# Attention in an encoder kernel: probabilities copied by DMA and transposed in float32r

## The chip, the cores and the metric

The kernel runs on one core of a Trainium2 chip. The metric is the device time of one execution in microseconds; the median of three runs before the change is 1133.47 us (1133.27 to 1133.87). The engines are named as in the profile: PE (matmuls), PEld (PE's weight loads), DVE (vector), ACT (scalar, activations), POOL (GpSimd), SP (issues most of the DMAs).

## The reference, cut to what matters

Two layers on 512 tokens of 1024 features, all float32. Layer 0 mixes with gated linear attention, layer 1 with softmax attention, and each is followed by a gated MLP with a width-3 convolution. The change lies in the softmax attention: 8 query heads of 128 features share 2 key/value heads, and 512 tokens are swept in 128-query blocks.

```
def block(q_blk):
    s = jnp.einsum('bkgqd,bksd->bkgqs', q_blk, k).astype(jnp.float32) * scale
    p = jax.nn.softmax(s, axis=-1).astype(v.dtype)
    return jnp.einsum('bkgqs,bksd->bkgqd', p, v)

o = lax.map(block, qb)
...
return o @ w_out
```

## The kernel before

Activations stay transposed in SBUF (features on partitions, 512 tokens along the row). Nearly every matmul is made of three float32r matmuls: each operand is split into a rounded high part (an ACT copy into a float32r tile) and a low part (a DVE subtraction of the high part from the value), and high x high, high x low and low x high are accumulated (`mm3`). Weights come in 1 MB pieces from DRAM through SP's queue into `raw` and are split into `wh` and `wl` by ACT and DVE; in the attention some low parts are made by an accumulating DMA on POOL's queue instead.

In `attention` the keys, the first pair of query heads and the values are projected first. Then a loop runs over t; step t does, in this order:

- `scores` of block t, where a block is one head and 128 queries: three matmuls into a bank tagged `s` (two banks), the row maximum `mx` and its negative scaled value `nb` on DVE, and the exponential on ACT, which writes `p` (128x512 float32, tag `t`, six buffers) and its row sums;
- some steps of the projection of the next pair of query heads (`qpair`, generators placed by the tables `Q_STEPS` and `Q_READY`) and of the output projection (`out_steps`, placed by `O_STEPS`);
- `turn` of block t - LAG: four 128x128 transposes on PE from `p` into a bank tagged `pt` (two banks); the high part `pth` by ACT, the low part `ptl` by DVE;
- `shares` of block t: the reciprocal of the row sums and the scaling of `p`, both on DVE;
- `mix` of the two blocks that end at t - LAG2, when that block is the second of a pair: twelve matmuls of 256 columns into `po`, and after a whole head the split of the result into `oT`.

LAGS is (4, 6). The tile framework then schedules the recorded instructions by its own cost estimates and writes each engine's order; so what stands in the order of the loop may be moved on an engine. It also chooses buffers and adds the waits. An instruction that waits on an engine holds back those behind it on that engine's queue; a DMA issued on ACT's queue is one of these.

`pe.transpose` makes the data the stationary operand and moves an identity matrix through it.

Of the kernel before, what the change touches and what calls it, by code (L numbers as in the profile page):

```python
# [8 lines left out]
F32 = mybir.dt.float32  # L9
F32R = mybir.dt.float32r  # L10
U8 = mybir.dt.uint8
AF = mybir.ActivationFunctionType
ALU = mybir.AluOpType

P = 128
S = 512
D = 1024
KC = D // P
NT = S // P
# [9 lines left out]

GATE_STEPS, GATE_LAG = (1, 3, 5, 7, 10, 12, 15, 17), 2  # L30

LAGS = (4, 6)

Q_STEPS = {1: (0, (4,) * 4), 2: (4, (3, 3, 2, 2, 2, 2, 2)), 3: (11, (2,) * 8)}
Q_READY = {1: (4, (3, 3, 2, 1, 1, 0, 1)), 2: (11, (3, 2, 2, 1, 1, 1, 0, 1)), 3: (19, (3, 2, 2, 1, 1, 1, 0, 1))}

O_STEPS = (22, 23, 25, 27, 29, 31, 32, 33, 34, 35, 36, 37)


PC_NORM = 0  # L40
# [6 lines left out]
def hybrid_encoder_kernel(  # L47
# [20 lines left out]
    nc = tc.nc  # L68
    pe, act, dve, pool, sync = nc.tensor, nc.scalar, nc.vector, nc.gpsimd, nc.sync
    mm = pe.matmul  # L70

    cp = ctx.enter_context(tc.tile_pool(name="cp", bufs=1))
    sp = ctx.enter_context(tc.tile_pool(name="sp", bufs=1))
# [4 lines left out]
    def nm(s):  # L78
        uid[0] += 1
        return f"{s}{uid[0]}"  # L80
# [3 lines left out]
    def bank(tag, n):  # L84
        return pp.tile([P, S], F32, tag=tag, bufs=PS[tag], name=nm(n))
# [4 lines left out]
    def big(dt, n):  # L90
        return pair("g", 22, dt, n)

    def tmp(tag, n, w=S):
        return sp.tile([P, w], F32, tag=tag, bufs={"u": 4, "t": 6, "sq": 3}[tag], name=nm(n))

    def tiny(w, n, tag="tiny"):
        return sp.tile([P, 8], F32, tag=tag, bufs={"tiny": 36, "tiny2": 4}[tag], name=nm(n))[:, :w]
# [73 lines left out]
        sync.dma_start(raw[c // 4][:, r], w_vg[c // 4, :, r])  # L171
        W.raw[id(w_vg), c // 4] = raw[c // 4]

    ident = cp.tile([P, P], F32, name="ident")
    make_identity(nc, ident)

    two = tmp("u", "two")
    dve.memset(two[:, :P], 2.0 ** -5)
# [85 lines left out]
    def mm3(ps, wh, wl, mh, ml, start, stop):  # L264

        mm(ps, wh, mh, start=start, stop=False)  # L266
        mm(ps, wh, ml, start=False, stop=False)  # L267
        mm(ps, wl, mh, start=False, stop=stop)  # L268
# [367 lines left out]
    def attention(norm, nxt):  # L636
# [22 lines left out]
        def roped(i, wcol, by, keep, tag="acc"):  # L659

            pa, pb = bank(tag, "A"), bank(tag, "B")
            yield from feature_steps(*W.half(qk_order[i], 0), norm.hl, pa)
            yield from feature_steps(*W.half(qk_order[i], 1), norm.hl, pb)
            qa, qb = tmp("sq", "qa"), tmp("sq", "qb")
            act.activation(qa, pa, AF.Square)
            act.activation(qb, pb, AF.Square)
            dve.tensor_tensor(qa, qa, qb, ALU.add)
            yield
            wa, wb = prm[:, wcol : wcol + 1], prm[:, wcol + 1 : wcol + 2]
            t = [tmp("u", "rt") for _ in range(4)]  # L670
            rt = ((t[0], pa, wa, cos), (t[2], pa, wa, sin), (t[1], pb, wb, sin), (t[3], pb, wb, cos))

            def turned(n):
                dst, src, w, tab = rt[n]
                dve.scalar_tensor_tensor(dst, src, w, tab, ALU.mult, ALU.mult)

            turned(0)
            yield
            sc = scale_tok(qa, by, keep)
            yield  # L680
            turned(1)
            yield
            turned(2)
            yield
            yield
            turned(3)
            yield
            res = big(F32, "ry")
            res = [res[:, :S], res[:, S:]]
            sub = dve if tag == "s" or keep == "ksc" else pool  # L690

            def head(e):
                r = slice(64 * e, 64 * e + 64)
                sub.tensor_tensor(res[e][0:64, :], t[0][r, :], t[1][r, :], ALU.subtract)
                pool.tensor_tensor(res[e][64:128, :], t[2][r, :], t[3][r, :], ALU.add)
                return res[e]

            return head, sc

        def split(y, tile_):  # L700
            act.activation(tile_[:, :S], y, AF.Copy)
            dve.tensor_tensor(tile_[:, S:], y, tile_[:, :S].bitcast(F32), ALU.subtract)
# [24 lines left out]
        def qpair(i, tag="acc"):  # L727
            head, sc = yield from roped(1 + i, PC_QK, float(HD), "qsc", tag)
            for e in range(2):
                y = head(e)  # L730
                yield
                t = big(F32R, "q")
                split(y, t)
                heads[2 * i + e] = (t, sc, e)
                yield
# [34 lines left out]
        probs, pts, pos = {}, {}, {}  # L770

        def scores(h, j):

            qt, sc, e = heads[h]
            kt = kk[h // 4]
            js = slice(j * P, (j + 1) * P)
            s = bank("s", "s")
            mm3(s, qt[:, js], qt[:, S + j * P : S + (j + 1) * P], kt[:, :S], kt[:, S:], True, True)
            scj = sc[:, 2 * j + e : 2 * j + e + 1]
            mx, nb, sm, rc = (tiny(1, n) for n in ("mx", "nb", "sm", "rc"))  # L780
            dve.reduce_max(mx, s, axis=mybir.AxisListType.X)
            dve.tensor_scalar(nb, mx, scj, -1.0, ALU.mult, ALU.mult)
            p = tmp("t", "p")
            act.activation(p, s, AF.Exp, scale=scj, bias=nb, accum_out=sm)
            probs[h, j] = (p, sm, rc)

        def shares(h, j):
            p, sm, rc = probs[h, j]
            dve.reciprocal(rc, sm)
            dve.tensor_scalar(p, p, rc, None, ALU.mult)  # L790
            probs[h, j] = p

        def turn(h, j):

            hf, i = divmod(j, 2)
            if i == 0:
                pts[h, hf] = tuple(big(F32R, n).rearrange("p (k q) -> p k q", q=256) for n in ("pth", "ptl"))
            ph3, pl3 = pts[h, hf]
            p = probs.pop((h, j))
            tp = bank("pt", "pt")  # L800
            for k in range(NT):
                pe.transpose(tp[:, k * P : (k + 1) * P], p[:, k * P : (k + 1) * P], ident)  # L802
            isl = slice(i * P, (i + 1) * P)
            tp3 = tp.rearrange("p (k q) -> p k q", q=P)
            act.activation(ph3[:, :, isl], tp3, AF.Copy)
            dve.tensor_tensor(pl3[:, :, isl], tp3, ph3[:, :, isl].bitcast(F32), ALU.subtract)

        def mix(h, hf):
            ph3, pl3 = pts.pop((h, hf))
            vo = (h // 4) * HD  # L810
            if hf == 0:
                pos[h] = bank("po", "po")
            dst = pos[h][:, hf * 256 : (hf + 1) * 256]
            for k in range(NT):
                vsl = slice(k * 256 + vo, k * 256 + vo + HD)
                mm3(dst, vh[:, vsl], vl[:, vsl], ph3[:, k, :], pl3[:, k, :], k == 0, k == NT - 1)
            if hf == 1:
                t = big(F32R, "oT") if h < 4 else pair("xhl", 8, F32R, "oT")
                split(pos[h], t)
                oh[h] = (t[:, :S], t[:, S:])  # L820

        LAG, LAG2 = LAGS
        blocks = [(h, j) for h in range(QH) for j in range(NT)]
        osteps = out_steps(w_aout, oh, nxt)
        plan = collections.defaultdict(list)
        for i in range(1, QH // 2):
            g = qpair(i)
            for first, counts in (Q_STEPS[i], Q_READY[i]):
                for t, n in enumerate(counts):
                    plan[first + t] += [g] * n  # L830
        for t in O_STEPS:
            plan[t].append(osteps)
        for t in range(len(blocks) + LAG2):
            if t < len(blocks):
                scores(*blocks[t])
            for g in plan[t]:
                next(g, None)
            if LAG <= t < len(blocks) + LAG:
                turn(*blocks[t - LAG])
            if t < len(blocks):  # L840
                shares(*blocks[t])
            if t >= LAG2:
                h, j = blocks[t - LAG2]
                if j % 2 == 1:
                    mix(h, j // 2)
# [3 lines left out]
    cw = gla(norms[0], norms[1])  # L849
    ffn(0, norms[1], cw, norms[2])  # L850
    attention(norms[2], norms[3])
    ffn(1, norms[3], cw, None)

# [80 lines left out]
```

## Time and profile before

| | before |
|---|---|
| median of 3 runs | 1133.47 us (1133.27 to 1133.87) |
| profiled execution: time, span | 1133.16 us, 1131.4 us |
| PE busy | 1125.7 us |
| PEld busy | 939.2 us |
| DVE busy | 690.1 us |
| ACT busy | 482.1 us |
| POOL busy | 76.0 us |
| first and last transpose of `p` start | 643.8 us, 734.2 us |
| first and last exponential start | 629.9 us, 726.5 us |

The profile is one execution. Busy times are the union of the instructions' durations on an engine; matmuls are pipelined, so several may be in flight, and a busy PE says that it always had one. The chain that ended last goes back from the last instruction, at each step to what released it, and so gives the time that each instruction added; in it a group of instructions shows the distance between starts rather than the duration. In a row of a group stand the line, engine, operation, output and inputs, shape and count, then busy time in us, mean ns of one, and the idle time of the engine before them with what ended it. In a row of the DMA issues stand the destination and source, the issuing queue, count, KB each and the median us from issue to landing.

### The profile page before, as it was taken

The page shows a single profiled execution, that of the slowest core. Times are in us where ns is not written, and L with a number is a line of the kernel's source. Part 1 is how long each engine was busy: PE and PEld are TensorE (multiplying, and loading weights), DVE is VectorE, ACT ScalarE, POOL GpSimd, SP SyncE. Part 2 cuts the span into 40 slices and gives each one's busy share as a digit, 9 for nine tenths or more (in the row PEclk, how much of TensorE's full clock was granted, in tenths as well). Part 3 has the DMA queues.
Part 4 walks back from the last instruction along what each step waited for, and adds up shares of the span by engine and source line. Part 5 has one row for each costly group of instructions (what it writes and reads, how often), then busy time and mean ns, then how long its engine had stood idle before and what let it go on. Part 6 is the DMA issues. An engine that isn't in the chain of part 4 may idle for free.

```text
span 1131.4 us, 12991 instructions
## 1 busy us (share of the span) xinstructions
PE 1125.7 (99%) x5260; PEld 939.2 (83%) x5260; DVE 690.1 (61%) x996; ACT 482.1 (43%) x690; POOL 76.0 (7%) x66
## 2 busy tenths in 40 slices
PE   9999999999999999999999999999999999999998
PEld 7888888888888888888888888888888888888887
DVE  6787563677777777633325589766777777762221
ACT  5564232444444444422234667644444444442210
POOL 0104110000000000000004433000000000000000
PEclk9999999999999999999999999999999999999999
DMA  6422211232322323223247633223232232323320
GB/s 231 149 75 78 84 63 38 75 112 75 112 97 90 112 75 112 100 86 112 77 152 181 149 76 75 56 75 112 75 112 85 101 112 75 112 84 121 130 93 19
DMA packets 19980, 111.66 MB, mean 99 GB/s; under 512 B 2384, under 2 KB 3024, under 8 KB 8400
## 3 DMA queue, kind: packets, MB, share of 16 engines
q1 hardware_dynamic: 17328, 102.29, 25.9%
q0 software_dynamic: 2304, 8.39, 3.9%
q8 instruction: 41, 0.67, 0.2%
q10 hardware_dynamic: 288, 0.15, 0.0%
q14 instruction: 19, 0.16, 0.0%
HBM read 100.34 MB, written 2.10 MB: 91 GB/s over the span
## 4 chain that ended last, share of the span: by engine, by line
PE 99%; DVE 0%; DMA 0%; ACT 0%; issue 0%; SPq 0%; DVEq 0%; ACTq 0%
PE up L266 14%; PE up L267 14%; PE up L268 14%; PE vg L297 8%; PE op L323 8%; PE dn L266 7%; PE dn L268 7%; PE dn L267 7%; PE o L548 2%; PE pt L802 1%; PE av L297 1%; PE kv L524 1%; PE A L266 1%; PE A L268 1%; PE A L267 1%; PE B L266 1%
## 5 line engine op out<-in xcount | busy, mean ns | idle before, releaser
L143 ACT ACTIVATE wh<-raw 128x1024 fp32r<-128x1024 f32 x164 | 173.3, 1056 | 351.4 <-PE up L267 132.8
L144 DVE TENSOR_TENSOR wl<-raw,wh 128x1024 fp32r<-128x1024 f32 x164 | 203.7, 1242 | 144.8 <-ACT wh L143 144.6
L266 PE MATMUL up<-xhl,wh 128*128 128x512 f32 x704 | 274.3, 390 | 0.0
L268 PE MATMUL up<-xhl,wl 128*128 128x512 f32 x704 | 273.9, 389 | 0.0
L267 PE MATMUL up<-xhl,wh 128*128 128x512 f32 x704 | 273.9, 389 | 0.0
L268 PEld LDWEIGHTS up<-xhl,wl 128*128 128x128 f32 x704 | 132.2, 188 | 27.6
L266 PEld LDWEIGHTS up<-xhl,wh 128*128 128x128 f32 x704 | 132.2, 188 | 27.4
L267 PEld LDWEIGHTS up<-xhl,wh 128*128 128x128 f32 x704 | 132.2, 188 | 27.1
L266 PE MATMUL dn<-gu,wh 128*128 128x512 f32 x352 | 136.9, 389 | 0.0
L267 PE MATMUL dn<-gu,wh 128*128 128x512 f32 x352 | 136.9, 389 | 0.0
L268 PE MATMUL dn<-gu,wl 128*128 128x512 f32 x352 | 136.9, 389 | 0.0
L603 DVE TENSOR_TENSOR u<-up,R 128x512 f32<-128x512 f32 x88 | 60.3, 687 | 52.7 <-PE up L268 52.7
L297 PE MATMUL vg<-wh,xhl 128*128 128x512 f32 x256 | 79.7, 390 | 0.6 <-DVE halfneg L184 0.6
L605 ACT ACTIVATE y<-u,cw 128x512 f32<-128x512 f32 x88 | 71.2, 811 | 20.4 <-DVE u L603 20.4
L268 PEld LDWEIGHTS dn<-gu,wl 128*128 128x128 f32 x352 | 66.1, 188 | 13.8
L267 PEld LDWEIGHTS dn<-gu,wh 128*128 128x128 f32 x352 | 66.1, 188 | 13.7
L266 PEld LDWEIGHTS dn<-gu,wh 128*128 128x128 f32 x352 | 66.1, 188 | 13.6
L323 PE MATMUL op<-oT,wh 128*128 128x512 f32 x256 | 70.9, 395 | 0.0
L607 DVE SCALAR_TENSOR_TENSOR y<-u,cw,y 128x511 f32<-128x511 f32 x88 | 65.9, 751 | 2.9
L606 DVE SCALAR_TENSOR_TENSOR y<-u,cw,y 128x511 f32<-128x511 f32 x88 | 65.6, 746 | 0.6 <-ACT y L605 0.6
L609 ACT ACTIVATE y<-y 128x512 f32<-128x512 f32 x44 | 27.9, 634 | 87.8 <-DVE y L607 87.8
L297 PEld LDWEIGHTS vg<-wh,xhl 128*128 128x128 f32 x256 | 48.0, 188 | 10.6 <-ACT sq L240 0.7
(186 smaller groups left out, 1432.1 us busy)
## 6 DMA issues: line engine op xcount, KB each, us to landing
raw<-in_w_up_dram SPq DMA_DIRECT2D x44, 1024.0 KB, 4.8
raw<-in_w_down_dram SPq DMA_DIRECT2D x22, 1024.0 KB, 4.8
wl<-raw POOLq DMA_DIRECT2D x16, 512.0 KB, 4.7
raw<-in_w_vg_dram SPq DMA_DIRECT2D x6, 1024.0 KB, 4.7
raw<-in_w_akq_dram SPq DMA_DIRECT2D x5, 1024.0 KB, 5.2
raw<-in_w_kq_dram SPq DMA_DIRECT2D x4, 1024.0 KB, 4.8
raw<-in_w_gout_dram SPq DMA_DIRECT2D x4, 1024.0 KB, 4.8
raw<-in_w_aout_dram SPq DMA_DIRECT2D x4, 1024.0 KB, 4.9
```

What stands on the lines that cost most here:

```text
L143: act.activation(hi[:, sl], r[:, sl], AF.Copy)
L144: dve.tensor_tensor(lo[:, sl], r[:, sl], hi[:, sl].bitcast(F32), ALU.subtract)
L266: mm(ps, wh, mh, start=start, stop=False)
L267: mm(ps, wh, ml, start=False, stop=False)
L268: mm(ps, wl, mh, start=False, stop=stop)
L297: mm(ps[j][:, :width], hl[k][i == 2][:, j * P : (j + 1) * P], (wl if i == 1 else wh)[:, sl], start=k == 0 and i == 0, stop=k == KC - 1 and ...
L323: mm(pss[ng][n], wt[:, sl], mv, start=k == 0 and i == 0, stop=k == KC - 1 and i == 2)
L603: dve.tensor_tensor(u, ps, norm.R, ALU.mult)
L605: act.activation(y, u, AF.Identity, scale=w(1), bias=w(3))
L606: dve.scalar_tensor_tensor(y[:, 1:], u[:, : S - 1], w(0), y[:, 1:], ALU.mult, ALU.add)
L607: dve.scalar_tensor_tensor(y[:, : S - 1], u[:, 1:], w(2), y[:, : S - 1], ALU.mult, ALU.add)
L609: act.activation(res[1], res[1], AF.Silu)
```

## The change

Five things change.

1. The identity is built in a temporary tile and copied by DVE into a float32r tile, `identr`; `ident` is now a float32 view of it.
2. After the scores of block t, a DMA on ACT's queue copies the scaled `p` of block t - 1 (256 KB) to a new tile of the same tag `t`, declared float32r and written through a float32 view, so that nothing is rounded. The six buffers of the tag now hold `p` and the copies.
3. The transposes read the copy and `identr` as float32r and write the bank through a float32r view.
4. For head 0 and head 4, first block each, the same copy is transposed a second time in float32 into a second `pt` bank; ACT copies it to SBUF, DVE subtracts the float32r transpose from it, and the difference times 2^20 is added to the low part `ptl`.
5. LAGS becomes (5, 7); the tables `Q_READY` and `O_STEPS` are moved, and the first step of each query projection is taken at the start of step 7, 15 or 23, ahead of the scores.

```diff
-LAGS = (4, 6)
+LAGS = (5, 7)
...
-Q_READY = {1: (4, (3, 3, 2, 1, 1, 0, 1)), 2: (11, (3, 2, 2, 1, 1, 1, 0, 1)), 3: (19, (3, 2, 2, 1, 1, 1, 0, 1))}
-
-O_STEPS = (22, 23, 25, 27, 29, 31, 32, 33, 34, 35, 36, 37)
+Q_READY = {1: (4, (3, 3, 2, 0, 1, 0, 1)), 2: (11, (3, 2, 2, 1, 0, 1, 0, 1)), 3: (19, (3, 2, 2, 1, 0, 1, 0, 1))}
+
+Q_FIRST = {1: 7, 2: 15, 3: 23}
+
+O_STEPS = (22, 23, 25, 27, 29, 31, 32, 34, 35, 36, 37, 38)
...
-    ident = cp.tile([P, P], F32, name="ident")
-    make_identity(nc, ident)
+
+    eye = tmp("sq", "eye")[:, :P]
+    make_identity(nc, eye)
+    identr = cp.tile([P, P], F32R, name="ident")
+    dve.tensor_copy(identr, eye)
+    ident = identr.bitcast(F32)
...
+        def copy(h, j):
+
+            t = sp.tile([P, S], F32R, tag="t", bufs=6, name=nm("pr"))
+            act.dma_start(t.bitcast(F32), probs[h, j])
+            probs[h, j] = t
+
...
-                pe.transpose(tp[:, k * P : (k + 1) * P], p[:, k * P : (k + 1) * P], ident)
+                pe.transpose(tp[:, k * P : (k + 1) * P].bitcast(F32R), p[:, k * P : (k + 1) * P], identr)
...
+            if h % 4 == 0 and j == 0:
+
+                tf = bank("pt", "ptf")
+                for k in range(NT):
+                    pe.transpose(tf[:, k * P : (k + 1) * P], p[:, k * P : (k + 1) * P].bitcast(F32), ident)
+                d = tmp("sq", "ptd")
+                act.activation(d, tf, AF.Copy)
+                dve.tensor_tensor(d, d, tp, ALU.subtract)
+                dve.scalar_tensor_tensor(pl3[:, :, isl], d.rearrange("p (k q) -> p k q", q=P), 2.0 ** 20,
+                                         pl3[:, :, isl].bitcast(F32), ALU.mult, ALU.add)
...
-        plan = collections.defaultdict(list)
+        plan, ahead = collections.defaultdict(list), {}
         for i in range(1, QH // 2):
             g = qpair(i)
+            ahead[Q_FIRST[i]] = g
...
+            if t in ahead:
+                next(ahead[t])
             if t < len(blocks):
                 scores(*blocks[t])
+            if 1 <= t <= len(blocks):
+                copy(*blocks[t - 1])
             for g in plan[t]:
                 next(g, None)
```

## The prediction

> **What bounds the kernel now.** I read the page first: span, busy shares, the chain that ended last. Then the stages between 645 and 705 us by windows, then the chain and the timeline of PE around the transposes.
>
> ```profile
> span 1131.4 us, 12991 instructions
> PE 1125.7 (99%) x5260; PEld 939.2 (83%) x5260; DVE 690.1 (61%) x996; ACT 482.1 (43%) x690; POOL 76.0 (7%) x66
> PEclk9999999999999999999999999999999999999999
> PE 99%; DVE 0%; DMA 0%; ACT 0%; issue 0%; SPq 0%; DVEq 0%; ACTq 0%
> ...
> 645.00:665.00 20.00, 20.00 (x112) 17.02 (x111) 15.36 (x35) 13.50 (x27) 6.51 (x6) 1.00 0.44 113
> 665.00:685.00 20.00, 20.00 (x122) 17.36 (x121) 17.20 (x38) 13.01 (x24) 8.95 (x7) 1.00 0.28 53
> 685.00:705.00 20.00, 19.74 (x130) 17.15 (x129) 17.67 (x41) 14.23 (x29) 7.87 (x6) 1.00 0.30 80
> ```
>
> PE is busy for 99% of the span and 99% of the last chain is PE, at the full granted clock. In the window rows (PE, PEld, DVE, ACT, POOL, clock, DMA share), which cover the attention blocks, PE never rests but for 0.26 us, DVE is 77 to 88% busy, ACT 65 to 71%. So a nanosecond of PE's stream is a nanosecond of the span, as long as DVE and ACT keep up; and DVE has the least room, in 685 to 705.
>
> What PE pays per instruction is the distance between starts, not the duration, since matmuls overlap. The chain gives it (start, us, what):
>
> ```profile
> 122.12 1.79 PE in L501 x16
> 662.64 0.44 PE pt L802 x4
> 667.06 0.86 PE hs L652 x8
> 740.11 27.23 PE op L323 x120
> ```
>
> Four float32 transposes cost 0.44 us: 110 ns each. A 512-column float32r matmul costs 27.23 / 120 = 227 ns. A 128-column float32 matmul stands as two records (L501, 64 records for 32 matmuls) of 1.79 / 16 = 112 ns. The hs matmuls move only 2 columns, and their records still cost 0.86 / 8 = 108 ns: that is what a load of 128 plain columns costs when nothing else hides it. For 256 columns of float32r, the timeline has twelve po matmuls from the first row to the second:
>
> ```profile
> 665.01 0.28 PE L266 MATMUL po<-pth,vh 128*128 128x256 f32 x1
> ...
> 666.43 0.40 PE L266 MATMUL s<-k,q 128*128 128x512 f32 x1
> ```
>
> That is 1.42 / 12 = 118 ns.
>
> **The change, part by part.**
>
> *The transposes (32 blocks of 4).* No float32r instruction of 128 columns is in the trace, so its price x is bounded. Below: 227 ns for 512 and 118 ns for 256 are 109 ns for 256 columns, so 118 - 55 = 64 ns for 128, an estimate. Above: the float32 transpose itself, 110 ns. The loads speak for some gain:
>
> ```profile
> L802 PE MATMUL pt<-ident,p 128*128 128x128 f32 x128 | 20.2, 273 | 0.0
> L802 PEld LDWEIGHTS pt<-ident,p 128*128 128x128 f32 x128 | 16.1, 141 | 4.0
> L267 PEld LDWEIGHTS po<-ptl,vh 128*128 128x128 f32 x64 | 12.2, 190 | 0.2
> ```
>
> A transpose's load lasts 141 ns where others last 190, so it may be cheap enough not to bind; but whether a float32r transpose keeps that load or takes the 190 ns one, no row shows. Neither end is nearer by any row, so I take the middle, 87 ns: 128 x (110 - 87) = 2.9 us saved (0 to 5.9). The Trainium skill, "TensorE: Matmul & The Clock Gate", section "Back-to-back issue gap", gives about 81 ns for a sustained 128-column pair; by it the saving would be an estimated 3.7 us. The same place gives 131 ns at 512 columns where this trace has 227, so I lean on it little.
>
> *The float32 copies of the transposes (blocks with h = 0 or 4, j = 0).* 8 more transposes at 110 ns on PE: +0.9 us. Each block also gets one ACT copy out of PSUM and two DVE operations. Their nearest rows:
>
> ```profile
> L805 ACT ACTIVATE pth<-pt 128x512 fp32r<-128x512 f32 x32 | 19.1, 597 | 19.9 <-PE pt L802 19.7
> L806 DVE TENSOR_TENSOR ptl<-pt,pth 128x512 fp32r<-128x512 f32 x32 | 21.9, 685 | 5.5 <-ACT pth L805 5.1
> L236 DVE SCALAR_TENSOR_TENSOR xhl<-x,prm,xhl 128x512 fp32r<-128x512 f32 x32 | 23.8, 748 | 8.2 <-ACT xhl L231 8.2
> ```
>
> So 0.60 us ACT and 0.69 + 0.75 = 1.43 us DVE per block. They also hold both pt banks at once: the next block's transposes must wait for the ACT copy of ptf, and the ones after them for the DVE subtraction, which reads tp. In the built order PE has 2.3 us of other work between ptf and the next transposes for the first block (six A matmuls and four of the scores), and 2.2 us for the second; pth and ptd need about 0.25 + 2 x 0.60 = 1.5 us, plus 0.4 us for a copy's issue between. It fits the first time. The second block falls near the place where DVE is already behind:
>
> ```profile
> 694.65 0.51 PE pt L802 x4
> 695.18 0.61 ACT pth L805
> 695.82 0.69 DVE ptl L806
> 698.40 0.59 DVE mx L781
> 698.99 1.05 DVE p L790
> 700.26 0.88 ACT p L784 x2
> 701.18 0.50 PE s L266
> ```
>
> Here the scores wait for an exponential that waits for a row of DVE work (0.26 us of PE lost). With 1.43 us more for DVE in each of two places, of which the two banks of s hide most, I put 0.5 us on PE (0 to 2.9: all of it uncovered).
>
> *The copies (32, one per block, on ACT's queue).* 256 KB from one tile to another. No such copy is in the trace; the nearest are:
>
> ```profile
> out_dram<-x SPq DMA_DIRECT2D x7, 256.0 KB, 2.1
> gconst<-in_scan_mask_dram SPq DMA_DIRECT2D x1, 256.5 KB, 3.2
> wl<-raw POOLq DMA_DIRECT2D x16, 512.0 KB, 4.7
> 1128.61 0.36 ACTq L633 DMA_DIRECT2D out_dram<-x  x1
> L784 ACT ACTIVATE p<-s,nb,qsc x32: 761/778/787, 629.9 to 726.5; 128x512 f32<-128x512 f32 x32
> L782 DVE TENSOR_SCALAR nb<-mx,qsc 128x1 f32<-128x1 f32 x32 | 6.7, 208 | 1.5 <-POOL qsc L656 1.3
> L789 DVE RECIPROCAL rc<-sm 128x1 f32<-128x1 f32 x32 | 5.2, 161 | 13.1 <-ACT p L784 12.5
> L790 DVE TENSOR_SCALAR p<-p,rc 128x512 f32<-128x512 f32 x32 | 17.4, 543 | 0.3
> 0.91 0.17 DVE L178 MEMSET two<- 128x128 f32 x1 [0.91 <-PEq L924]
> ```
>
> The issue holds ACT's sequencer for 0.36 us; it stands behind the exponential of the next block (0.78 us), under which it can hide, so ACT loses between 0 and 32 x 0.36 = 11.5 us of its 29% idle time. In the built order most copies wait for the copy before to land: six buffers hold p and its copy, and a copy goes into the buffer that the last one emptied. Behind the waiting copy stand, on ACT, pth of an older block, oT, the q splits and the next exponential; PE's scores wait for the latter. The exponentials come every (726.5 - 629.9) / 31 = 3.1 us. A landing of 2.1 us is over before the next copy is issued; 3.2 us would be level with it; 4.7 us would pace the loop (a rival below). I take 2.1 us, because that row has the size and the quiet queues that most of this stage has (DMA share 0.28 to 0.44): nothing. The use comes four steps after the copy, 12 us, so PE does not wait for it; in the tail the built order has some 10 us of matmuls between the last scores and the last transposes, against mx, nb, exponential, reciprocal, scaling (0.6 + 0.2 + 0.9 + 0.2 + 0.5 us, the first and third from the chain above) and a copy (2.1 us).
>
> *The rest.* Moving the projections and output steps by one place keeps their count on PE; zero, covered by the two s banks and by LAG one larger. The identity goes through a copy on DVE at the start (about 0.2 us, as the 128x128 memset of the last row, 0.17), after DVE's first weight split; between 0 and 0.2, I take 0.
>
> **The sum.** -2.9 + 0.9 + 0.5 = -1.5 us. Against the profiled execution (1133.16 us, of which 1131.4 span) that is 1131.66; the median of the runs, 1133.47, lies 0.31 above it, so 1131.9 us.
>
> **The rivals.**
>
> *A, the stream binds (x = 64 ns).* The 141 ns load supports it. -5.9 + 0.9 + 0.5 = -4.5: 1129.0 us; with nothing lost to DVE, 1128.5.
>
> *C, nothing is gained (x = 110).* The change would not do what it says: the load of 128 columns binds, as it does for hs at 108 ns, or the transpose moves its columns alike for both types. +0.9 + 0.5 = 1.4: 1134.9 us, within noise of slower. Against it stands the shorter load of transposes. The Trainium skill, same page, section "LDWEIGHTS (loading the stationary operand)", gives columns / 1.2 ns, 107 ns for 128; the hs row agrees, so by this rule no float32r pair of 128 columns gets below 107 ns.
>
> *D, the copies pace ACT: the slower side.* Place: the copy's wait for its predecessor. It decides once a copy takes over 3.1 us. At 4.7 us each of some ten copies that meet weight loads (645 to 665 us: DMA share 0.44) adds up to 1.6 us, of which about 3 us in all (the two s banks) are hidden: +13 at most; at 3.7 us +3. With the middle, 8, less the sum's 1.5: 1140 us. For it: the akq, aout and wl transfers run in this stage. Against: at share 0.44 the engines are free more than half the time.
>
> *E, float32r is slow at 128 columns.* If it falls back to the two records of a float32 matmul, 224 ns: 128 x 114 = 14.6, with 0.9 and 0.5 for the rest 1149.5 us. Nothing in the trace speaks for it except that no float32r matmul here is narrower than 256.
>
> **Chances.** The forecast 0.34, A 0.28, C 0.16, D 0.14, E 0.08. About 0.2% (2.3 us) is what a measurement of this kernel can tell from no change, so faster means under 1131.2: nearly all of A and a third of the forecast's case (x below 80 ns, or no loss on DVE), 0.38. Same: the rest of the forecast's case and most of C, 0.33. Slower: D, E and C with a larger loss on DVE, 0.29. The range 1128.5 to 1138.5 takes in A, the forecast, C and half of D. The forecast's own range is 1130 to 1134.
>
> **What would show it.** The distance of four pt transposes in the chain: 0.35 us (0.26 for A, 0.44 for C, 0.9 for E). ptf groups of 0.44 us, two of them. A landing time for pr<-p at 2.1 us, and no wait of ACT's queue on DMA longer than a few tenths. PE idle in the attention stage below 1 us, and where it is, released by ACT p or DVE. The forecast is wrong if x lies at an end, or if ACT's waits for pr appear in the chain.

## The result, and the profile after

The changed kernel takes 1138.67 us (median of 3 runs, 1137.44 to 1140.03), against 1133.47 before: a ratio of 1.0045, 95% interval 1.0031 to 1.0059. It is 5.2 us slower where 1.6 us faster was forecast, and lies 0.2 us above the range. The profiled execution took 1140.03 us, the slowest of the three, so its trace shows 1.4 us more loss than the median run has. The mean granted clock was 1.000 in the run of 1137.44 us, and 0.998 and 0.999 in the other two.

The page of the changed kernel: span, busy times, the chain that ended last by engine.

```profile
span 1138.3 us, 13118 instructions
...
PE 1126.9 (99%) x5268; PEld 939.4 (83%) x5268; DVE 693.6 (61%) x1001; ACT 482.2 (42%) x692; POOL 75.9 (7%) x66
...
PE 95%; DMA 2%; DVE 1%; ACT 1%; issue 0%; ACTq 0%; DVEq 0%
```

PE was 99% of the chain and is 95%; DMA, DVE and ACT have entered it. The busy shares hardly move, so the stage has to be looked at. First its ends, by the instructions of the tiles `s` and `op`, before and after (line, engine, operation, count, shortest/median/longest ns, first and last start):

```profile
L266 PE MATMUL s<-k,q x32: 389/476/504, 625.4 to 722.9; 128*128 128x512 f32 x32
L323 PE MATMUL op<-oT,wl x128: 388/389/400, 184.9 to 766.9; 128*128 128x512 f32 x128
```

```profile
L272 PE MATMUL s<-k,q x32: 387/396/502, 625.7 to 729.7; 128*128 128x512 f32 x32
L329 PE MATMUL op<-oT,wl x128: 388/389/399, 185.3 to 773.8; 128*128 128x512 f32 x128
```

From the first scores to the last output projection it was 766.9 - 625.4 = 141.5 us and is 148.1 us. What follows lasts 364.5 us in both. Of the 6.9 us by which the span of this execution is longer, 6.6 us lie in the attention loop.

The windows of the stage after the change (PE, PEld, DVE, ACT, POOL, granted clock, DMA share, GB/s):

```profile
645.00:665.00 20.00, 16.65 (x86) 13.40 (x85) 13.28 (x28) 9.67 (x20) 6.93 (x6) 0.91 0.48 140
665.00:685.00 20.00, 19.46 (x120) 16.48 (x118) 15.02 (x35) 12.88 (x26) 7.72 (x6) 1.00 0.65 182
685.00:705.00 20.00, 19.74 (x128) 17.09 (x128) 18.09 (x43) 14.01 (x27) 5.13 (x5) 1.00 0.55 167
705.00:725.00 20.00, 19.03 (x125) 16.20 (x124) 18.53 (x43) 13.28 (x27) 4.01 (x3) 1.00 0.34 110
725.00:745.00 20.00, 18.82 (x117) 15.80 (x116) 12.35 (x26) 10.31 (x19) 0.88 (x1) 1.00 0.47 147
```

PE is idle for 100 - 93.70 = 6.30 us of these 100. In the same windows of before it was idle 0.26 us: the prediction shows the first three, and these are the other two:

```profile
705.00:725.00 20.00, 20.00 (x121) 16.48 (x120) 16.76 (x42) 13.95 (x29) 0.92 (x1) 1.00 0.29 79
725.00:745.00 20.00, 20.00 (x115) 17.07 (x115) 9.45 (x16) 7.94 (x14) 0.00 (x0) 1.00 0.00 1
```

Half of the 6.30 us is in the first window, where the clock also fell to 0.91. The chain (start, us, what) says what ended the idle time, and what a transpose now costs:

```profile
643.51 8.03 DMA pr<-p
...
651.62 0.52 ACT p L790
...
663.81 0.31 PE pt L814 x4
...
668.65 5.93 DMA pr<-p
...
692.57 5.24 DMA pr<-p
```

Four transposes take 0.30 us (0.29 to 0.31 where PE is not waiting), 75 ns each; before it was 110. On PE, that part of the change gives 128 x 35 ns = 4.5 us. Three copies stand in the chain with landings of 5 to 8 us. The shortest, median and longest landing of `pr`:

```profile
DMA to landing us min/median/max: 2.2/2.3/8.0
```

The median is near the forecast's 2.1 us. The tail is not: each of the three was issued 0.5 to 0.6 us after a 1 MB weight load, and the copy of 643.51 also just after an accumulating 512 KB transfer on POOL's queue:

```profile
642.93 0.33 SPq L120 DMA_DIRECT2D raw<-in_w_aout_dram  x1
643.31 0.86 POOL L135 DMA_DIRECT2D wl<-raw  x1 [5.99 <-ACT wl L126]
643.51 0.47 ACTq L802 DMA_DIRECT2D pr<-p  x1
...
651.62 0.78 ACT L790 ACTIVATE p<-s,nb,qsc 128x512 f32<-128x512 f32 x1 [7.85 <-DMA pr<-p]
651.67 0.47 ACTq L802 DMA_DIRECT2D pr<-p  x1
```

The waits of the stage (engine and line, what ended the wait, us in total, times, longest):

```profile
ACT p L790 <- DMA pr<-p: 11.3, 2, 7.9
...
PE s L272 <- ACT p L790: 3.6, 3, 2.9
```

In the built order this exponential stands ahead of the next copy, which is issued at 651.67. So it is the exponential itself that waits for the landing, for 7.9 us, probably because it writes into the buffer that the late copy still reads; PE's scores wait for the exponential. The copy of 668.65 holds an exponential in the same way. The copy of 692.57 holds the next copy, issued at 697.83, and a weight split behind it on ACT's queue. The timeline of PE shows the price of the first one, and a second price behind it:

```profile
652.54 0.50 PE L272 MATMUL s<-k,q 128*128 128x512 f32 x1 [2.88 <-ACT p L790]
653.52 0.54 PE L814 MATMUL pt<-ident,pr 128*128 128x128 f32 x4 [0.47 <-ACT ptd L825]
...
655.49 0.63 PE L272 MATMUL B<-xhl,wh 128*128 128x512 f32 x1
655.91 0.63 PE L273 MATMUL B<-xhl,wh 128*128 128x512 f32 x1
...
658.40 0.40 PE L272 MATMUL B<-xhl,wh 128*128 128x512 f32 x1
658.63 0.40 PE L273 MATMUL B<-xhl,wh 128*128 128x512 f32 x1
...
710.20 0.36 PE L814 MATMUL pt<-ident,pr 128*128 128x128 f32 x2 [0.97 <-DVE ptl L818]
```

Some 2 us after the rest of 2.88 us, matmuls start 0.43 us apart, then 0.23 again: from 654.68 to 658.10 the granted clock is 0.50, which costs about half of these 3.4 us, 1.7 us. The wait for `ptd` is for the second `pt` bank, which the float32 transposes hold until ACT has copied it, and ACT was late. At 710.20, after the second such block, a transpose waits for DVE, which from 699.9 us on has gone from one operation to the next without a pause.

In sum: 6.6 = -4.5 (transposes) + 0.9 (eight more) + 10.2 lost to waits. Of these the rows show 6.0 us of idle and 1.7 of clock. The rest, 2.5 us, is probably short gaps: a matmul's record is 0.39 us long where starts are 0.23 apart, so the first 0.16 us of each gap does not count as idle.

### The profile page after: what moved, and what is told of

It is laid out like the page before. It is cut to its first block, busy times and chain, and to the rows that moved or that the text cites. A ratio compares the mean times of both kernels' runs of the same rounds, so it can differ in the third digit from the quotient of the medians.

```text
span 1138.3 us, 13118 instructions
## 1 busy us (share of the span) xinstructions
PE 1126.9 (99%) x5268; PEld 939.4 (83%) x5268; DVE 693.6 (61%) x1001; ACT 482.2 (42%) x692; POOL 75.9 (7%) x66
## 4 chain that ended last, share of the span: by engine, by line
PE 95%; DMA 2%; DVE 1%; ACT 1%; issue 0%; ACTq 0%; DVEq 0%
PE up L273 14%; PE up L272 14%; PE up L274 14%; PE vg L303 8%; PE op L329 7%; PE dn L272 7%; PE dn L273 7%; PE dn L274 7%; DMA pr<-p 2%; PE o L554 2%; PE av L303 1%; PE kv L530 1%; PE B L272 1%; PE B L273 1%; PE B L274 1%; PE k L274 1%
```

## The experiments

Four theories. 1: copies land late beside weight loads, and through the shared six buffers a late one blocks ACT. 2: the second transposes with their DVE work, in a stage where DVE has least room. 3: the moved order. 4 (formed after the first runs): the copy's issue on ACT, which waits for the scaling of `p`, stands between two exponentials. Where a time is measured against the kernel before, that one ran on the same chip (medians of 1133.25 to 1133.43 us).

**Own buffers for the copies.**

```diff
-            t = sp.tile([P, S], F32R, tag="t", bufs=6, name=nm("pr"))
+            if j % 2 == 0:
+                cps[h] = big(F32R, "pr")
+            t = cps[h][:, j % 2 * S : (j % 2 + 1) * S]
```

> The changed kernel, but the copies go into buffers of their own (two copies in one tile of the tag g) instead of the six buffers that also hold p, so that a copy no longer waits for the copy before it to land. Theory 1 (the late landings of a few copies, 5 to 8 us beside weight loads, hold ACT's queue through the shared buffers): the copies land as late as before, but ACT's waits on pr<-p shrink from 11.3 us to under 3, PE's idle time in 625 to 745 us falls from 6 us to under 2, and the time is 1130 to 1132 us. Theory 2 (the two float32 blocks cost it, by banks and DVE work): unchanged, 1138 us. Theory 3 (the moved tables cost it): unchanged, 1138 us.

Measured: 1141.09 us, ratio 1.0065 (1.005 to 1.008). ACT no longer waits for `pr`, yet nothing is gained: the idle time has moved to 705 to 725 us, where PE is busy for 16.22 of 20 us. But this edit changed more than the wait. The framework wrote another order on ACT: by the timelines a copy is now issued ahead of the exponential of the next block (by over 0.3 us) in 25 of 31 cases, where in the changed kernel it is in 4, and within 0.2 us of the end of its scaling in 28 of 32 cases, where it was in 4. So the run does not show what the wait is worth by itself.

**Without the second transposes.** The eight transposes, two ACT copies and four DVE operations go; the term they add is zero in exact arithmetic.

```diff
-            if h % 4 == 0 and j == 0:
-                tf = bank("pt", "ptf")
...
```

> The changed kernel without the second, float32 transposes of two blocks and without their difference (the output leaves out that term). Theory 1: only their own work goes, 0.9 us of PE and what they add to DVE: 1136.5 to 1138 us, ACT's waits on pr<-p still about 11 us. Theory 2: most of the loss goes, 1130 us. Theory 3: 1137.5 us.

Measured: 1133.91 us, ratio 1.0006 (0.9996 to 1.0015). So these two blocks cost 4.8 us, five times their 0.9 us on PE. The order of copies and exponentials on ACT is nearly that of the changed kernel (5 of 31 copies ahead). The late copy is still there, with the first of these waits; PE's longest rest is now shorter, and the clock stays at 1.00:

```profile
ACT p L790 <- DMA pr<-p: 6.4, 1, 6.4
```

```profile
650.61 0.50 PE L272 MATMUL s<-k,q 128*128 128x512 f32 x1 [1.56 <-ACT p L790]
```

**Float32 transposes of the copies**, the rest as in the changed kernel.

```diff
-                pe.transpose(tp[...].bitcast(F32R), p[...], identr)
+                pe.transpose(tp[...], p[...].bitcast(F32), ident)
```

> The changed kernel with the transposes of the copies read as float32 instead of float32r; all else stays. Four of them should stand 0.44 us apart in the chain instead of 0.30. Theory 1 with a gain of 35 ns per transpose: at most 128 x 0.035 = 4.5 us slower, less what PE's waits swallow, 1141 to 1143 us. If float32r brings nothing: 1138.5 us.

Measured: 1141.44 us, ratio 1.0067 (1.005 to 1.0084), 2.8 us above the changed kernel. Here four stand 0.44 us apart again, so the float32r transposes save 4.5 us on PE, of which 2.8 us arrive in this comparison.

**Rounded probabilities, no copy.** The kernel before, with the scaling on DVE writing a float32r tile directly; the low part of the probabilities is lost.

```diff
-            dve.tensor_scalar(p, p, rc, None, ALU.mult)
+            t = sp.tile([P, S], F32R, tag="t", bufs=6, name=nm("pr"))
+            dve.tensor_scalar(t, p, rc, None, ALU.mult)
```

> The kernel before, with its tables and no copy, where DVE's scaling writes the probabilities rounded to float32r and the transposes run in float32r (their low part is lost, so the result is less exact). It shows the price of float32r alone. If a transpose takes 75 ns instead of 110 and PE stays the bound: 1133.5 - 4.5 = 1129 us, PE idle below 1 us. If DVE or ACT becomes the bound in this stage, 1130 to 1132 us with idle PE before the scores.

Measured: 1131.06 us, ratio 0.9979 (0.9969 to 0.9988): 2.3 us faster, with nothing but the transposes changed in kind. Even here half of the 4.5 us is not had. The chain has DVE in it, where the kernel before had next to none:

```profile
669.69 1.56 DVE pr L794
...
675.06 1.48 DVE pr L794
```

With PE shorter per block, DVE and ACT set the pace in places. The two scalings shown are stretched ones, beside `ry` operations on POOL; the median scaling of this run takes 0.48 us.

**The order alone.** The kernel before with the new tables, LAGS and step ahead; no copies, float32 transposes.

```diff
-LAGS = (4, 6)
+LAGS = (5, 7)
...
-Q_READY = {1: (4, (3, 3, 2, 1, 1, 0, 1)), ...
+Q_READY = {1: (4, (3, 3, 2, 0, 1, 0, 1)), ...
```

> The kernel before with the moved tables, LAGS (5, 7), the step taken ahead and the float32r identity alone: no copies, float32 transposes, no second transposes. If the order itself costs nothing (as predicted): 1133.4 +- 1 us, PE idle in 645 to 745 us below 1 us. If the moved order is what the 2 us between the gain of the transposes and the run without the second transposes were lost to: 1135 us or more, with PE idle near 650 and 680 us without any copy.

Measured: 1135.9 us, ratio 1.0028 (1.0017 to 1.004): the order costs 2.5 us by itself. A window in which PE was never idle before:

```profile
665.00:685.00 20.00, 18.74 (x114) 15.77 (x114) 16.56 (x37) 12.19 (x23) 8.74 (x7) 1.00 0.23 44
```

```profile
666.85 1.02 PE L658 MATMUL hs<-bd,qa 128*128 128x2 f32 x8 [0.97 <-DVE nb L788]
```

The `hs` matmuls of a projection now wait for the sum of squares `qa`, which the new order puts on DVE behind `ptl`, a scaling, `oT` and a row maximum. Which of the moves costs how much was not separated.

**Own buffers, without the second transposes.**

```diff
+            t = cps[h][:, j % 2 * S : (j % 2 + 1) * S]
...
-            if h % 4 == 0 and j == 0:
-                tf = bank("pt", "ptf")
...
```

> Copies into tiles of their own (no copy waits for the landing before it), and the second transposes with their difference left out (that term is zero in exact arithmetic). Theory 1 (late landings through the shared six buffers): the wait of ACT's queue on pr<-p goes, with it the 2.5 us of PE idle near 650 and 680 us, 1131 us or less. Theory 4 (the issue of a copy, 0.47 us, and its wait for the scaling of p stand between two exponentials on ACT): the idle moves to other places and stays above 1.5 us, 1132.5 to 1134 us.

Measured: 1138.69 us, ratio 1.0047 (1.0034 to 1.0059). With own buffers it is 4.8 us slower than with the shared ones, where theory 1 expected a gain. The chain from 717.99 us shows a closed loop of ACT and DVE in which PE does not appear:

```profile
717.99 0.41 DVE p L796
718.47 0.47 ACTq L806
719.04 0.88 ACT p L790 x2
719.94 0.16 DVE rc L795
720.11 0.36 DVE mx L787
720.47 0.15 issue
720.61 0.68 DVE ptl L822
721.29 0.40 DVE p L796
...
```

Scaling, copy's issue, next exponential, its scaling: 3.3 us a turn, no shorter than the 3.1 us between exponentials before. ACT is not full (11.13 of 20 us), but its order is fixed, and in that order a copy that waits for a scaling holds the exponential that DVE is waiting for. This is the order written for own buffers: 24 of 31 copies are issued ahead of the next exponential, and 31 of 32 within 0.2 us of the end of their scaling, where in the run with shared buffers these were 5 and 2. So the loop fits this run and the first one; of the changed kernel, where most copies stand behind the exponential, it says little, and what late landings cost there stays open.

**The same, each copy one step later**, so that its scaling is a whole step old.

```diff
-            if 1 <= t <= len(blocks):
-                copy(*blocks[t - 1])
+            if 2 <= t <= len(blocks) + 1:
+                copy(*blocks[t - 2])
```

> As the run before it (own buffers, second transposes left out), but step t copies block t - 2 instead of t - 1, so that the scaling that a copy waits for is a whole step old. Theory 4: no DVE p in front of a copy's issue on the chain, PE idle in 645 to 745 us below 1 us, 1129 to 1130.5 us (the whole 4.5 us of the transposes). Theory 1 or 3 (tables): no faster than the run before it, within 0.5 us.

Measured: 1136.37 us, ratio 1.0023 (1.0014 to 1.0032), 2.3 us better than the run before it, in the direction of theory 4, but far from 1130. Part of the distance is the clock: the two of its eleven runs at a granted clock of 1.000 took 1133.24 and 1133.97 us, the nine at 0.997 or 0.998 took 1135.7 to 1137.4. The forecast for it overlooked that a later copy is also nearer to its use. One that landed in 5.6 us met a waiting transpose:

```profile
717.90 5.61 DMA pr<-p
```

```profile
723.65 0.51 PE L818 MATMUL pt<-ident,pr 128*128 128x128 f32 x4 [2.83 <-DMA pr<-p]
```

The clock of the window from 725 us was 0.92, lowered as after the 2.88 us above.

**Weight loads in quarters**, shared buffers, without the second transposes.

```diff
-                sync.dma_start(t, src[i])
+                for q in range(n):
+                    w = 4 * S // n
+                    sync.dma_start(t[:, q * w : (q + 1) * w], src[i, :, q * w : (q + 1) * w])
```

> Copies in the shared six buffers as in the changed kernel, second transposes left out; each 1 MB weight load of the attention is issued as four loads of a quarter of the columns (2 KB rows instead of 8 KB). If a copy is late because its packets take turns with packets four times as long, its landing beside a load falls from 6 to 8 us to 3 to 4 us, no ACT wait on pr<-p above 1 us, and the time is that of own buffers without second transposes. If the copy is late because of the engines' bandwidth alone, the landing stays at 5 us or more and the time at 1133.9 us or above.

Measured: 1133.01 us, ratio 0.9996 (0.9987 to 1.0005), against 1133.91 without the split; the longest landing is 6.0 us where it was 7.0. Neither expectation holds: the length of the weight loads' rows has a part in the late landings, not the larger one. Its eleven runs spread from 1131.3 to 1135.5 us, and the three longest, 1134.6 us and more, are those at a granted clock of 0.998. In the profiled one of them PE's longest rest ends at 664.80, and the clock of the window from 665 to 685 us is 0.91:

```profile
664.80 1.02 PE L661 MATMUL hs<-bd,qa 128*128 128x2 f32 x8 [1.51 <-DVE rc L798]
```

The rest of 1.56 us in the run without the split left the clock at 1.00. So the length of a rest does not decide alone whether the clock falls after it.

**The order of before, with the copies**, without the second transposes: the tables and the loop of before put back.

```diff
-LAGS = (5, 7)
+LAGS = (4, 6)
...
-            if t in ahead:
-                next(ahead[t])
```

> Float32r transposes of copies in the shared six buffers, second transposes left out, but with the tables, LAGS (4, 6) and the order of the kernel before. Theory 3 (the moved order costs 2.5 us by itself, as the run of the tables alone gave, and the sum of parts holds): 1133.9 - 2.5 = 1131.4 us. Rival (the copies need the larger lag, and the order is only bad without them): 1134 us or more, with PE's transposes waiting for pr<-p.

Measured: 1132.04 us, ratio 0.9989 (0.9981 to 0.9998). The order costs 1.9 us with the copies too, and the copies don't need the larger lag: no transpose waits for `pr`. Against the rounded run, which has the same tables and no copies, it is 1.0 us slower.

**The copies on SP's queue**, shared buffers, without the second transposes.

```diff
-            act.dma_start(t.bitcast(F32), probs[h, j])
+            sync.dma_start(t.bitcast(F32), probs[h, j])
```

> As the run without second transposes (1133.9 us), but the copies are issued on SP's queue, which carries the weight loads, and not on ACT's. If the issue on ACT (0.47 us) and its waits for the scaling and for the landing before it are what delays the exponentials: no wait of ACT's exponential on pr<-p and none on the scaling, PE idle in 645 to 745 us down by 2 us, 1131.5 to 132 us. If the shared buffers and the late landings delay it, whoever issues: 1133.5 us or more.

Measured: 1144.13 us, ratio 1.0095 (1.0081 to 1.0108). A clear miss, 10.2 us slower than with the copies on ACT's queue: behind the weight loads the copies are worse off. Their median landing is 3.2 us, the exponential still waits for them through the shared buffers, and one of them holds PE:

```profile
ACT p L790 <- DMA pr<-p: 11.4, 2, 5.8
...
PE pt L814 <- DMA pr<-p: 3.2, 1, 3.2
```

**Second transposes without their DVE work.** Transposes and ACT copies stay; the difference and the sum go.

```diff
-                dve.tensor_tensor(d, d, tp, ALU.subtract)
-                dve.scalar_tensor_tensor(pl3[:, :, isl], d.rearrange(...), 2.0 ** 20, ...)
```

> The changed kernel with the second transposes and their ACT copy, but without the two DVE operations (difference and sum; that term is zero in exact arithmetic). If DVE's 1.4 us in each of two places make the 4.8 us: 1134.8 us (the run without second transposes plus 0.9 us for eight transposes). If the held pt bank and the ACT copy make it: 1137.5 us or more, and PE still idles near 650 us for 2 us or more.

Measured: 1134.42 us, ratio 1.0014 (1.0005 to 1.0023): 0.5 us above the run without the blocks, 4.2 us below the changed kernel. So the cost of the blocks lies in DVE's work, 2 x 1.4 us by the rows of before, and not in the bank that ACT's copy holds: the wait of 0.47 us for `ptd` is still in this run. The subtraction on DVE also keeps the other bank longer, and the run does not separate that from the time that it takes on DVE.

**The changed kernel in the order of before.**

```diff
-LAGS = (5, 7)
+LAGS = (4, 6)
...
-            if t in ahead:
-                next(ahead[t])
             if t < len(blocks):
                 scores(*blocks[t])
             if 1 <= t <= len(blocks):
                 copy(*blocks[t - 1])
```

> The changed kernel with only the tables, LAGS (4, 6) and the order of the loop as in the kernel before; copies and both second transposes with their DVE work are kept. If the parts add: 1132.0 + 4.8 = 1136.8 us. If the vector work costs only in the moved order: 1133.5 us or less. If the shorter lag makes it worse, since the two checked blocks then hold the banks closer to their use: 1138.5 us or more.

Measured: 1135.6 us, ratio 1.0022 (1.0013 to 1.0031). In this order the blocks cost 3.6 us, with a granted clock of 1.000 in all eleven runs; in the moved order they cost 4.8. So they cost in either. PE waits at the second one, first for the bank that the subtraction holds:

```profile
701.32 0.54 PE L812 MATMUL pt<-ident,pr 128*128 128x128 f32 x4 [0.52 <-DVE ptd L824]
...
705.10 0.54 PE L812 MATMUL pt<-ident,pr 128*128 128x128 f32 x4 [1.10 <-DVE ptl L816]
```

**One of the two blocks**, in two kernels, the second with `h == 4`.

```diff
-            if h % 4 == 0 and j == 0:
+            if h == 0 and j == 0:
```

> The changed kernel with the second transposes and their DVE work for head 0 alone (the term left out for head 4 is zero in exact arithmetic). If both places cost alike: 1133.9 + 2.4 = 1136.3 us. If it is the place of head 4, where DVE is busiest (685 to 725 us): below 1135 us. If it is the place of head 0, where the late copy lies: above 1137.5 us.

> The changed kernel with the second transposes and their DVE work for head 4 alone. If both places cost alike: 1136.3 us. If it is the place of head 4: above 1137.5 us. If it is the place of head 0: below 1135 us.

Measured: 1135.3 us, ratio 1.0023 (1.0014 to 1.0032), for head 0; 1136.04 us, ratio 1.0033 (1.0022 to 1.0043), for head 4. They cost 1.4 and 2.1 us, and both together 4.8. The clock is the likely reason for the last 1.3 us. By the runs at a granted clock of 1.000 alone, the single blocks cost 1.2 us (six runs) and 2.1 us (four runs), and both together 1137.44 - 1133.91 = 3.5 us, which is about their sum and the 3.6 us of the order of before; but the changed kernel has only one such run. The lowered clock comes with a single block too, in 4 of 11 and 2 of 7 runs, and in 5 of the 11 runs without the DVE work.

**The order of before, weight loads in quarters**, without the second transposes.

```diff
-LAGS = (5, 7)
+LAGS = (4, 6)
...
-                sync.dma_start(t, src[i])
+                for q in range(n):
```

> The order of before, copies in the shared buffers, no second transposes, and the 1 MB weight loads of the attention as four loads of a quarter of the columns. If late landings still cost in this order: 0.9 us less than the same without the split, as it was in the moved order: 1131.1 us. If they are covered by then: 1132.0 us.

Measured: 1131.38 us, ratio 0.9984 (0.9976 to 0.9993), faster than both kernels and 0.7 us less than the same without the split, a difference that the intervals (0.9976 to 0.9993 and 0.9981 to 0.9998) do not quite tell apart. It leaves the extra term out.

**The rotation `ry` on DVE instead of POOL**, in the changed kernel.

```diff
-            sub = dve if tag == "s" or keep == "ksc" else pool
+            sub = dve
...
-                pool.tensor_tensor(res[e][64:128, :], t[2][r, :], t[3][r, :], ALU.add)
+                dve.tensor_tensor(res[e][64:128, :], t[2][r, :], t[3][r, :], ALU.add)
```

> The changed kernel with all ry operations (the rotation of the query heads, 12 of them in the loop, 1.33 us each on POOL) on DVE instead of POOL. If POOL's ry makes the scalings beside it long: none of the 32 scalings of p above 0.55 us in this stage except beside qsc, and neither of the two sums ptl<-ptd,ptl above 0.75 us (they take up to 1.97 and 1.17 us in the changed kernel). If something else does (the copies' reads of p, the DMA traffic): scalings of 0.9 us and more remain. The time: DVE gets 12 x 0.68 = 8.2 us more and loses about 4 us of stretching, in a stage where DVE has least room, so no faster than 1138.7 us, up to 1143 us.

Measured: 1138.44 us, ratio 1.0051 (1.0034 to 1.0067), the time of the changed kernel. The scalings of `p` and the sums `ptl<-ptd,ptl`, first in the changed kernel, then in this one (shortest/median/longest ns):

```profile
L796 DVE TENSOR_SCALAR p<-p,rc x32: 472/478/1965, 631.7 to 734.4; 128x512 f32<-128x512 f32 x32
...
L827 DVE SCALAR_TENSOR_TENSOR ptl<-ptd,ptl x2: 681/924/1167, 655.0 to 706.8; 128x512 fp32r<-128x512 f32 x2
```

```profile
L796 DVE TENSOR_SCALAR p<-p,rc x32: 474/478/488, 630.8 to 730.2; 128x512 f32<-128x512 f32 x32
...
L827 DVE SCALAR_TENSOR_TENSOR ptl<-ptd,ptl x2: 681/682/683, 649.8 to 702.5; 128x512 fp32r<-128x512 f32 x2
```

Beside POOL's `ry` a scaling takes up to 1.97 us (the longest stands beside `qsc` on POOL as well); with `ry` gone from POOL none takes over 0.49. The Trainium skill, "SBUF — State Buffer", section "Who interferes with whom", lists `tensor_scalar` among the operations with which DVE can take the pair of ports that it shares with GpSimd, and says that whichever issues first gets the pair for the whole instruction. These runs agree, with 1.97 and 0.49 us. What DVE wins it probably gives back by doing the twelve rotations itself (0.68 us each), hence no change in time.

## Why the prediction was wrong, point by point

The medians give a sum of parts, in the order in which they were taken off:

| part | predicted | measured |
|---|---|---|
| 128 transposes in float32r | -2.9 (0 to -5.9) | -4.5 on PE |
| moved order | 0 | +2.5 (tables alone) |
| copies, and what of the 4.5 is not had | 0 | +2.5 (1133.91 less 1135.9 - 4.5) |
| two float32 blocks | +0.9 + 0.5 (0.5: 0 to 2.9) | +4.8 |
| sum | -1.5 | +5.3; run: +5.2 |

The last row is no test, since parts that are taken off one after another add up to the run by construction. And the third row is not the price of the copies: the rounded run has none and still has only 2.3 of the 4.5 us.

- *What bounds the kernel.* Right for the kernel before, and the condition was written down ("as long as DVE and ACT keep up"). It failed at once: with DVE 77 to 88% busy, a PE that is 0.14 us shorter per block lets DVE and ACT into the chain. The rounded run, which adds no instruction to the loop, shows it: 2.3 us of 4.5.
- *The price x of a transpose.* 87 ns was taken as the middle of 64 and 110; it is 75. The term was mis-sized by 1.6 us, on the side of a gain. Rival C, which took an estimated 107 ns for a load of 128 columns, by the rule of the Trainium skill, "TensorE: Matmul & The Clock Gate", section "LDWEIGHTS (loading the stationary operand)", as the least distance of two transposes, is refuted by the 75 ns; the 81 ns of its section "Back-to-back issue gap" were nearer than the middle. Rival E is refuted too.
- *The step that failed most: "I put 0.5 us on PE (0 to 2.9: all of it uncovered)".* The two blocks' DVE work costs 4.2 us (1138.67 - 1134.42), where 0.5 was put and 2.9 was the bound. By the runs at a granted clock of 1.000 alone it is 3.4 us, with one run of the changed kernel. In the order of before, where no run shows a lowered clock, the blocks cost 3.6 us with their transposes, 2.7 without the 0.9 of these. So about all of the 2.9 us came through: the step that failed is that the two banks of `s` would hide most of it. At the second block DVE runs without a pause from 699.9 us until the transpose at 710.20 has waited for it. On top comes the lowered clock, 1.7 us in the profiled execution, for which the prediction has no term. The durations were also those of quiet rows: beside POOL's `ry` the sum takes up to 1.2 us and a scaling up to 1.97 us.
- *"I take 2.1 us [...]: nothing" for the copies.* The median landing was nearly right, the tail was not: 5 to 8 us behind a weight load. That is what rival D said, with its victims, the exponential and then the scores. Its place, the copy's wait for its predecessor, fits one of the three late copies; behind the two others the exponential itself waits for the landing. What these waits cost in all stays open, since the runs with own buffers changed the order on ACT as well. Two figures bear on it: in the order of before the kernel with copies is 1.0 us slower than the rounded one without (1132.04 and 1131.06), and weight loads in quarters bring 0.9 and 0.7 us; all three differences are hardly beyond the intervals. That the issue "stands behind the exponential of the next block" was right for 27 of 31 blocks of the changed kernel; the loop of scaling, issue and exponential, 3.3 us a turn, rules where it stands ahead, with own buffers.
- *"Moving the projections [...]: zero, covered by the two s banks and by LAG one larger".* Wrong by 2.5 us (1.9 with the copies). The cover named was for the scores; in the run of the tables alone `hs` waits 0.97 us and a q split 0.3 us for DVE work that the new order puts later, and no bank covers these.
- *The start-up identity* cost nothing that shows: the first scores start at 625.7 us instead of 625.4, and at 625.1 and 625.6 in two other runs with the new identity.
- *What would show it.* The list was right in what it asked: four transposes at 0.30 us, PE idle 6.3 us instead of below 1, and "ACT's waits for pr appear in the chain". A granted clock below 1.00 was not on it.

The forecast of 1131.9 us is 1131.66 + 0.31 = 1131.97, a slip of rounding. Without the moved order and the two blocks the prediction's terms leave 1133.5 - 2.9 = 1130.6 us; that kernel takes 1132.0. That this is near is partly luck: the saving on PE is 1.6 us larger than forecast, but 2.2 us of it is not had even without copies, and with the copies it is another 1.0 us slower, where nothing was forecast.

## What to carry to other kernels

Where PE is busy for 99% and another engine for 85% of a stage, a saving on PE can be worth much less than its size (2.3 of 4.5 us here); look for the loop through the other engines (here maximum, exponential, scaling, issue) and compare its length with PE's time per block. A DMA issued on a compute engine's queue is an instruction of that engine: what it waits for, the engine waits for. Small work added to the engine with least room can cost its whole duration, and more where PE's rests lower the clock, and a moved order should be run by itself before the rest is judged. An edit that frees buffers can change the order that the framework writes: compare the orders of the two runs before a difference in time is put down to the buffers.

## What the runs showed of the hardware

- A float32r transpose of 128x128 costs 75 ns between starts, a float32 one 110; their loads last 143 ns in the one and 141 in the other.
- A copy of 256 KB from SBUF to SBUF lands in 2.2 us at the least, 2.3 in the median, and in 5 to 8 us when it is issued 0.5 to 0.6 us after a 1 MB load; its issue on ACT takes 0.47 us, where the write to DRAM in the prediction took 0.36.
- After rests of PE of 2.88, 2.83 and 1.51 us the granted clock was 0.50 for 3.4 us, with matmuls 0.43 instead of 0.23 us apart after the first; after one of 1.56 us it stayed at 1.00. The same kernel shows the lowered clock in some runs and not in others.
- A scaling on DVE takes 0.48 us, and 0.9 to 1.97 us beside POOL's rotations; with these moved to DVE, none takes over 0.49 us.
